# Sample scores of a decoder step: four products with a running sum against one product and one sum along the last axis, and combined output weights made inside the heads' part

## The chip, the cores and the metric

The kernel runs on one core of a Trainium2 chip. The metric is the device time of one execution in microseconds (us). Engines are called as in the profile: PE is the matrix engine, PEld its weight load, DVE the vector engine, ACT the scalar engine, POOL the general one, and SP the engine from whose queue nearly all DMAs are issued. Each engine works through its own list of instructions in order; semaphores hold an instruction back until what it reads is there and what it overwrites has been read.

## The reference

One layer of a hybrid decoder: eight heads of stick-breaking attention and four groups of gated linear attention (GLA) share one input projection and one output projection. There are 1072 tokens: 16 learned meta tokens, a prompt of 1024, and 32 sample tokens (8 sequences of 4). Cut to what the change touches:

```python
def branch_inputs(h, w_in, w_alpha, b_alpha):
    u = h @ w_in
    sq, sk, sv, sg, gq, gk, gv, gg, ga = jnp.split(u, idx, axis=-1)
    ...
    log_f = jax.nn.log_sigmoid((ga @ w_alpha + b_alpha).astype(jnp.float32)) / GLA_TAU

def sb_sample(q, k_new, v_new, k_past, v_past, bias):
    z = jnp.concatenate([sb_logits(q, k_past, bias), sb_logits(q, k_new, bias)], axis=-1)
    ...

def branch_output(o_sb, sg, o_gla, gg, gla_norm_g, w_out):
    ...
    mixed = jnp.concatenate([o_sb * jax.nn.silu(sg), o_gla * jax.nn.silu(gg)], axis=-1)
    return mixed @ w_out
```

`sb_logits(q, k_past, ...)` is the dot product of each sample query (4 tokens in each of 8 sequences and 8 heads, 128 elements) with the 1024 past keys of its sequence. The keys lie in a paged cache: 8 pages of 128 keys for each sequence. So there are 8 heads x 8 sequences x 8 pages = 512 pieces of 128 keys x 128 elements, each met by four queries.

## The kernel before

**Projections.** The fp32 products run as three products of a high and a low part each (L288, L289, L290 in `inproj`). A projection of 128 columns takes eight weight chunks; `weight_chunk` (L176) loads a chunk by a DMA on SP (`wr`, L179), ACT rounds it to the high part (`wh`, L183) and DVE subtracts to get the low part (`wl`, L184), with three buffers each. Each chunk then feeds three column chunks of 384, 384 and 304 tokens with six matmuls each, 18 in all, into three PSUM accumulators (`accp`, three buffers for the whole program, so that a new projection's first matmul waits until ACT or DVE have copied out the old accumulator).

**Order.** The projections are the backbone. After each group of six matmuls `inproj` calls `W.beat()`: the `Weaver` advances every generator that is due, a generator writes a few instructions and yields the number of beats until it is due again. Afterwards a tile scheduler makes each engine's list out of the dependencies, its own modelled times and the priority of each instruction; weight chunks and the evacuation of accumulators are written under `urgent()`. `spread` (and the same lines inside `z_feed`) gives an instruction an ordering dependency, without a semaphore, on the last matmul written (`W.mark`), so that it isn't scheduled much earlier than written.

**Stages**, by the profiled execution: input, norm and transposes until about 75 us; the heads' part until about 790 us (for each of eight heads the projections v, k and q, and the attention over the prompt); `low_rank` (L314), the 16-column projection `ga` that the GLA decays are made of; the gates; the four GLA groups g from about 883 to 1385 us, each with the projections gk, gq, gv_0 and gv_1; more gates; around 1472 to 1720 us the sample tokens' softmax and values with the last gates; and the output projection until the end. Of the GLA part the prediction speaks of: the decay's stage (`al`, `ny`, `e`, L727 to L737), the evacuation of `acc_gk` (L672 to L680) and of `acc_gv` (L684 to L693, into `graw`), the product of `gk` with its decay (L825), and four transposes of it at a time (`tr_k`, L859) which ACT copies to `kd` (L864).

**The two generators of the change** are spawned once head 0 has its projections and run beside everything else:

- `z_feed` (L351) makes the sample scores. For each of the 512 pieces a page `kp` (128 keys x 128 elements) is loaded, up to six ahead into seven buffers, and for each sequence and head the four queries are loaded to all partitions (`qb`, 128 x 4 x 128). Four DVE instructions multiply the page by one query each and sum along the elements at the same time (L386, `accum_out`); the product itself (`jk`) is thrown away. The profile shows each as two rows: the multiplication and a read of the accumulator. A piece every two beats.
- `weight_forms` (L402) makes four of the "combined" weights of the output projection, which multiplies quarters of the matrix in seven products: in 16 tiles `tf` (128 x 4 x 512, one buffer) four DMAs load pieces of the four quarters of `w_out` (L407), four DVE subtractions combine them in place (L411), four DMAs store them to memory (`td`, L414). The yields make 60 beats for each tile, 960 in all. `td` is read again from 1854 us on (L1307).

Of the kernel before, what the change touches and what calls it, by code (L numbers as in the profile page):

```python
# [10 lines left out]
F32 = mybir.dt.float32  # L11
F32R = mybir.dt.float32r
# [4 lines left out]
ALU = mybir.AluOpType  # L17
# [3 lines left out]
P = 128  # L21
# [5 lines left out]
NT = 4  # L27
NSMP = NB * NT
T = META + SEQ + NSMP
# [5 lines left out]
NPG = 8  # L35
# [47 lines left out]
def hybrid_step(ctx: ExitStack, tc: tile.TileContext, x_prompt, x_sample, cache_k, cache_v, state_gla,  # L83
# [23 lines left out]
    W = Weaver()  # L107
# [188 lines left out]
    dk_cm = tc.tile_pool(name="dk", bufs=2, side="right")  # L296
    dk = dk_cm.__enter__()
    wa = []
    ga = dk.tile([96, T], F32R, tag="ga", bufs=1, name="ga")
    walr = dk.tile([96, GH * P], F32, tag="walr", bufs=1, name="walr")  # L300

    def low_rank_weights():
# [11 lines left out]
    def low_rank():  # L314

        acc = [accp.tile([P, 512], F32, tag="acc", name=f"acc_ga_{c}") for c in range(3)]
        for kb in range(0, NK, 4):
            for c, (lo, hi) in enumerate(CHUNKS):
                n = hi - lo
                for k in range(kb, kb + 4):  # L320
                    mm(acc[c][:32, :n], wa[k // 8][:, k % 8, :], hh[k][:, lo:hi], start=(k == 0), stop=False)
                    mm(acc[c][:32, :n], wa[k // 8][:, k % 8, :], hl[k][:, lo:hi], start=False, stop=(k == NK - 1))
                W.beat()
            W.beat()
        for c, (lo, hi) in enumerate(CHUNKS):
            with urgent():
                ps = acc[c][:32, :hi - lo]
                act.copy(ga[0:32, lo:hi], ps)
                act.copy(ga[64:96, lo:hi], ps)
                vec.tensor_tensor(ga[32:64, lo:hi], ps, ga[0:32, lo:hi].bitcast(F32), ALU.subtract)  # L330

    paged = {}

# [11 lines left out]
        done.append(d.ins)  # L345


    heads_ready = []
    z_done = set()

    def z_feed(rate):  # L351

        def pages():
            for h in range(HEADS):
                for b in range(NB):
                    for i in range(NPG):
                        yield h, b, i
        qbs, kps = {}, {}

        def fetch(h, b, i):  # L360
            if i == 0:
                qbs[h, b] = dk.tile([P, NT, P], F32, tag="qb", bufs=2, name=f"qb{b}_{h}")
                nc.sync.dma_start(qbs[h, b][:], qsd[b * NT:(b + 1) * NT, h * P:(h + 1) * P].partition_broadcast(P))
            kps[h, b, i] = dk.tile([P, P], F32, tag="kp", bufs=7, name=f"kp{b}_{h}_{i}")
            page_dma(kps[h, b, i][:], cache_k, b, i, slice(h, h + 1))

        ahead = pages()
        fetched = 0
        zt = None
        for n, (h, b, i) in enumerate(pages()):  # L370
            while h not in heads_ready:
                yield 4
            while fetched < n + 6:
                nx = next(ahead, None)
                if nx is None or nx[0] not in heads_ready:
                    if nx is not None:
                        ahead = itertools.chain([nx], ahead)
                    break
                fetch(*nx)
                fetched += 1  # L380
            if i == 0:
                zt = dk.tile([P, NT, NPG], F32, tag="zt", name=f"zt{b}_{h}")
            kp = kps.pop((h, b, i))
            for t in range(NT):
                jk = dk.tile([P, P], F32, tag="jk", bufs=1, name=f"jk{b}_{h}_{i}_{t}")
                ins = vec.scalar_tensor_tensor(jk[:], kp[:], 1.0, qbs[h, b][:, t, :], ALU.mult, ALU.mult,  # L386
                                         accum_out=zt[:, t, NPG - 1 - i:NPG - i])
                if t == 0 and W.mark is not None:
                    tc.add_manual_dep(ins.ins, W.mark.name, NOSYNC, reason="spread")
            if i == NPG - 1:  # L390
                nc.sync.dma_start(zd[b][:, h * 32:(h + 1) * 32], zt[:].rearrange("p a r -> p (a r)"))
                if h == HEADS - 1:
                    z_done.add(b)
            yield rate(n)

    def spread(ins):

        if W.mark is not None:
            tc.add_manual_dep(ins.ins, W.mark.name, NOSYNC, reason="spread")


    def weight_forms():  # L402
        for k, q in itertools.product(range(8), range(2)):
            t = dk.tile([P, 4, 512], F32, tag="tf", bufs=1, name=f"tf{k}_{q}")
            for i, (r, c) in enumerate(((0, 0), (0, 1), (1, 1), (1, 0))):
                r0, c0 = 1024 * r + k * P, 1024 * c + q * 512
                spread(nc.sync.dma_start(t[:, i, :], w_out[0, r0:r0 + P, c0:c0 + 512]))  # L407
                yield 4
            yield 12
            for i, a, b in ((0, 1, 0), (1, 1, 2), (2, 2, 0), (3, 3, 2)):  # L410
                spread(vec.tensor_tensor(t[:, i, :], t[:, a, :], t[:, b, :], ALU.subtract))  # L411
                yield 4
            for j, i in enumerate((0, 2, 1, 3)):
                spread(nc.sync.dma_start(td[j][:, k, q * 512:(q + 1) * 512], t[:, i, :]))  # L414
                yield 4


    def gate_rest(g, lo, hi, x):
# [226 lines left out]
    with tc.tile_pool(name="gp", bufs=1) as gp, tc.tile_pool(name="gps", bufs=1, space=PSUM) as gps:  # L645
# [73 lines left out]
        def decay(g, cb):  # L719

            gs = slice(g * P, (g + 1) * P)
            raw = walr[:, gs]
            wal = gp.tile([96, P], F32R, tag="wal", name=f"wal{g}")
            act.copy(wal[:], raw)
            vec.tensor_tensor(wal[64:96, :], raw[64:96], wal[64:96, :].bitcast(F32), ALU.subtract)
            for c, (lo, hi) in enumerate(CHUNKS):
                n = hi - lo  # L727
                yield 5
                ps = gps.tile([P, 512], F32, tag="P", bufs=2, name=f"al{g}_{c}")
                mm(ps[:, :n], wal[:], ga[:, lo:hi], start=True, stop=True)  # L730
                ny = stage(f"ny{g}_{c}")[:, :n]
                e = stage(f"e{g}_{c}")[:, :n]
                act.activation(ny, ps[:, :n], AF.Identity, scale=-1.0, bias=nbal[:, g:g + 1])
                vec.tensor_scalar(e, ny, 30.0, None, ALU.min)
                act.activation(e, e, AF.Exp)
                act.activation(e, e, AF.Ln, bias=1.0)
                vec.tensor_tensor(e, ny, e, ALU.max)  # L737
                for i in range(3):
                    a = i * P
                    w = P if 3 * c + i < 8 else 16  # L740
                    k = 3 * c + i
                    out = view(cb, col(k) + (P - 1 if k % 2 else 0), (-1 if k % 2 else 1, w))
                    vec.tensor_tensor_scan(out, ones[:].to_broadcast([P, w]), e[:, a:a + w], 0.0, ALU.mult, ALU.add)
                if hi > REAL:
                    vec.tensor_tensor_scan(cb[:, REAL:T], sm4[:], e[:, REAL - lo:], 0.0, ALU.mult, ALU.add)
                yield 1
# [817 lines left out]
```

## Time and profile before

| | us |
|---|---|
| median of three runs | 2112.36 |
| the three runs | 2115.4, 2111.5, 2112.36 |
| the profiled execution: its own time | 2108.24 |
| its span in the trace | 2106.5 |
| from its first to its last instruction of `weight_forms` (L407 to L414) | 87.4 to 1320.9 |
| mean granted clock of PE in it | 0.995 |

The profile is of one execution, so a sum of its parts is to be set against 2108.24 or 2106.5, not against the median. How busy the engines are in each fortieth of the span (53 us), in tenths, shows where each stage has its limit:

```profile
PE   5999999999999999999999999999999999999998
DVE  6368888889888889899889988877544347453576
ACT  7346555565655547423535335353444326332342
DMA  6234443544444353544353444434776666352485
```

PE is busy in 9 tenths or more of every slice but the first and the last. DVE stands at 8 or 9 tenths while the generators run, and falls to 3 to 7 behind them. A wait is shown as engine, tile, line, "<-" and what ended it, then total us, number and longest us. A row of the timeline is start, duration, engine, line, operation, output<-inputs, shapes, and in brackets the idle time before it and what ended it.

### The profile page before, as it was taken

Reading aid. Unit: us, or ns where it says so; the run is one execution under the profiler, and the core shown is the slowest. Engines: PE = TensorE matmul, PEld = TensorE weight load, DVE = VectorE, ACT = ScalarE, POOL = GpSimd, SP = SyncE. Lnnn points to the kernel's source line nnn. Section 1 sums busy time; section 2 is a strip of 40 time slices with the busy share of each in tenths; the row PEclk is TensorE's granted clock in tenths of the full one; section 3 lists DMA queues with packets and bytes.
Section 4 is the critical chain, followed back from the end, with each engine's and each line's share of the span. In section 5 each row is a group of like instructions: output and inputs, shape, how many; then the busy total and the mean of one; then the engine's idle time right before and its main releaser. Section 6 shows DMA issues by size and latency. Waiting matters only on the chain.

```text
span 2106.5 us, 43298 instructions
## 1 busy us (share of the span) xinstructions
PE 2056.2 (98%) x12546; PEld 1868.4 (89%) x12546; DVE 1569.7 (75%) x6593; ACT 991.8 (47%) x2539; POOL 80.9 (4%) x298
## 2 busy tenths in 40 slices
PE   5999999999999999999999999999999999999998
PEld 4999999999999989999899898998888888777776
DVE  6368888889888889899889988877544347453576
ACT  7346555565655547423535335353444326332342
POOL 0000000100000000020000000000000000000000
PEclk9999999999999999999999999999999999999999
DMA  6234443544444353544353444434776666352485
GB/s 200 72 103 123 132 131 100 144 118 121 139 124 126 108 145 102 156 132 117 110 138 104 123 129 113 107 85 135 244 234 219 224 218 201 127 159 75 130 279 186
DMA packets 378505, 301.96 MB, mean 143 GB/s; under 512 B 50073, under 2 KB 318777, under 8 KB 378265
## 3 DMA queue, kind: packets, MB, share of 16 engines
q1 hardware_dynamic: 376072, 298.91, 48.1%
q8 instruction: 99, 1.62, 0.3%
q14 instruction: 142, 1.16, 0.2%
q10 hardware_dynamic: 2192, 0.27, 0.1%
HBM read 241.75 MB, written 57.31 MB: 142 GB/s over the span
## 4 chain that ended last, share of the span: by engine, by line
PE 84%; DMA 6%; DVE 6%; ACT 2%; issue 1%; SPq 0%; DVEq 0%; POOL 0%; ACTq 0%; POOLq 0%
PE acc_g L288 4%; PE acc_g L290 4%; PE b L1471 4%; PE acc_g L289 4%; PE b L1472 4%; PE b L1473 4%; PE acc_k L288 3%; PE acc_gv L288 3%; PE acc_k L289 3%; PE acc_q L288 3%; PE acc_k L290 3%; PE acc_gv L290 3%; PE acc_gv L289 3%; PE acc_q L289 3%; PE acc_q L290 3%; PE acc_v L288 3%
## 5 line engine op out<-in xcount | busy, mean ns | idle before, releaser
L386 DVE SCALAR_TENSOR_TENSOR jk<-kp,qb 128x128 f32<-128x128 f32 x2048 | 591.6, 289 | 38.9 <-DMA qb<-qsd 1.5
L288 PE MATMUL acc_g<-hT,wh_g 128*128 128x368 f32 (+2 forms) x768 | 251.7, 328 | 0.8 <-ACT gx L442 0.8
L290 PE MATMUL acc_g<-hT,wl_g 128*128 128x368 f32 (+2 forms) x768 | 248.4, 323 | 0.0
L289 PE MATMUL acc_g<-hT,wh_g 128*128 128x368 f32 (+2 forms) x768 | 247.9, 323 | 0.0
L1471 PE MATMUL b<-ring,f 128*128 128x512 f32 x416 | 165.7, 400 | 3.2 <-ACT b L1344 2.0
L386 DVE DVE_READ_ACCUMULATOR jk<-kp,qb 128x1 f32 x2048 | 166.9, 81 | 0.0
L1309 DVE TENSOR_TENSOR ring<-wr,ring 128x512 fp32r<-128x512 f32 x104 | 70.6, 690 | 128.7 <-ACT ring L1308 128.3
L1472 PE MATMUL b<-ring,f 128*128 128x512 f32 x416 | 162.8, 391 | 0.7 <-DVE ring L1309 0.5
L1473 PE MATMUL b<-ring,f 128*128 128x512 f32 x416 | 162.4, 390 | 0.0
L288 PEld LDWEIGHTS acc_g<-hT,wh_g 128*128 128x128 f32 x768 | 145.1, 189 | 12.4 <-issue 10.2
L290 PEld LDWEIGHTS acc_g<-hT,wl_g 128*128 128x128 f32 x768 | 144.9, 189 | 2.0 <-issue 2.0
L289 PEld LDWEIGHTS acc_g<-hT,wh_g 128*128 128x128 f32 x768 | 145.1, 189 | 0.7
L1308 ACT CAST ring<-wr 128x512 fp32r<-128x512 f32 x104 | 64.4, 622 | 159.0 <-DMA wr<-in_w_out_dram 80.6
L288 PE MATMUL acc_gv<-hT,wh_gv 128*128 128x384 f32 (+1 forms) x384 | 129.6, 338 | 0.0
L288 PE MATMUL acc_k<-hT,wh_k 128*128 128x378 f32 (+1 forms) x384 | 127.8, 333 | 0.0
L288 PE MATMUL acc_q<-hT,wh_q 128*128 128x368 f32 (+2 forms) x384 | 125.5, 327 | 0.0
L289 PE MATMUL acc_k<-hT,wh_k 128*128 128x378 f32 (+1 forms) x384 | 125.5, 327 | 0.0
L290 PE MATMUL acc_k<-hT,wl_k 128*128 128x378 f32 (+1 forms) x384 | 125.3, 326 | 0.0
L290 PE MATMUL acc_gv<-hT,wl_gv 128*128 128x384 f32 (+1 forms) x384 | 125.2, 326 | 0.0
L289 PE MATMUL acc_gv<-hT,wh_gv 128*128 128x384 f32 (+1 forms) x384 | 124.6, 325 | 0.0
L289 PE MATMUL acc_q<-hT,wh_q 128*128 128x368 f32 (+2 forms) x384 | 123.8, 322 | 0.0
L290 PE MATMUL acc_q<-hT,wl_q 128*128 128x368 f32 (+2 forms) x384 | 123.6, 322 | 0.0
(441 smaller groups left out, 5398.3 us busy)
## 6 DMA issues: line engine op xcount, KB each, us to landing
kp<-in_cache_k_dram SPq DMA_DIRECT2D x512, 64.0 KB
vr<-in_cache_v_dram SPq DMA_DIRECT2D x64, 512.0 KB
tf<-in_w_out_dram SPq DMA_DIRECT2D x64, 256.0 KB
qb<-qsd SPq DMA_DIRECT2D x64, 256.0 KB
td<-tf SPq DMA_DIRECT2D x64, 256.0 KB
wr_g<-in_w_in_dram SPq DMA_DIRECT2D x128, 128.0 KB
wr<-td SPq DMA_DIRECT2D x64, 256.0 KB
wr<-in_w_out_dram SPq DMA_DIRECT2D x48, 256.0 KB
```

The source lines that it names most:

```text
L288: mm(acc[c][:, :n], wh[:, k2, :], hh[k][:, lo:hi], start=(k == 0), stop=False)
L289: mm(acc[c][:, :n], wh[:, k2, :], hl[k][:, lo:hi], start=False, stop=False)
L290: W.mark = mm(acc[c][:, :n], wl[:, k2, :], hh[k][:, lo:hi], start=False, stop=(k == NK - 1)).ins
L386: ins = vec.scalar_tensor_tensor(jk[:], kp[:], 1.0, qbs[h, b][:, t, :], ALU.mult, ALU.mult, accum_out=zt[:, t, NPG - 1 - i:NPG - i])
L1308: act.copy(wh, r)
L1309: vec.tensor_tensor(wl, r, wh.bitcast(F32), ALU.subtract)
L1471: mm(bk[:], ah, wh, start=first and k == 0, stop=False, skip_group_check=True)
L1472: mm(bk[:], ah, wl, start=False, stop=False, skip_group_check=True)
L1473: mm(bk[:], al, wh, start=False, stop=last and k == 7, skip_group_check=True)
```

## The change

Three things change, with no other line of the kernel.

1. A page's four multiplications with running sum become one DVE multiplication of the page, repeated along a middle axis, with all four queries (`jk` is now 128 x 4 x 128), and one DVE reduction of `jk` along its last axis into the page's column of `zt`. The reads and writes in memory are the same.
2. `weight_forms` yields 2 beats behind each load, subtraction and store instead of 4, and 8 instead of 12 between the loads and the subtractions: 32 beats for each tile, 512 in all. Its loads, subtractions and stores are the same in number and size.
3. `ga` no longer has a buffer of its own: when `weight_forms` has ended, `ga` is allocated in the buffer of `tf`, and `low_rank` runs beats until that has happened before it copies its accumulators out.

```diff
-    ga = dk.tile([96, T], F32R, tag="ga", bufs=1, name="ga")
...
     def low_rank():
...
+        while not ga:
+            W.beat()
+        g = ga[0]
         for c, (lo, hi) in enumerate(CHUNKS):
             with urgent():
                 ps = acc[c][:32, :hi - lo]
-                act.copy(ga[0:32, lo:hi], ps)
-                act.copy(ga[64:96, lo:hi], ps)
-                vec.tensor_tensor(ga[32:64, lo:hi], ps, ga[0:32, lo:hi].bitcast(F32), ALU.subtract)
+                act.copy(g[0:32, lo:hi], ps)
+                act.copy(g[64:96, lo:hi], ps)
+                vec.tensor_tensor(g[32:64, lo:hi], ps, g[0:32, lo:hi].bitcast(F32), ALU.subtract)
...
+    ga = []
...
             kp = kps.pop((h, b, i))
-            for t in range(NT):
-                jk = dk.tile([P, P], F32, tag="jk", bufs=1, name=f"jk{b}_{h}_{i}_{t}")
-                ins = vec.scalar_tensor_tensor(jk[:], kp[:], 1.0, qbs[h, b][:, t, :], ALU.mult, ALU.mult,
-                                         accum_out=zt[:, t, NPG - 1 - i:NPG - i])
-                if t == 0 and W.mark is not None:
-                    tc.add_manual_dep(ins.ins, W.mark.name, NOSYNC, reason="spread")
+            jk = dk.tile([P, NT, P], F32, tag="jk", bufs=1, name=f"jk{b}_{h}_{i}")
+            spread(vec.tensor_tensor(jk[:], kp[:].unsqueeze(1).to_broadcast([P, NT, P]), qbs[h, b][:], ALU.mult))
+            vec.tensor_reduce(zt[:, :, NPG - 1 - i:NPG - i], jk[:], mybir.AxisListType.X, ALU.add)
...
                 spread(nc.sync.dma_start(t[:, i, :], w_out[0, r0:r0 + P, c0:c0 + 512]))
-                yield 4
-            yield 12
+                yield 2
+            yield 8
             for i, a, b in ((0, 1, 0), (1, 1, 2), (2, 2, 0), (3, 3, 2)):
                 spread(vec.tensor_tensor(t[:, i, :], t[:, a, :], t[:, b, :], ALU.subtract))
-                yield 4
+                yield 2
             for j, i in enumerate((0, 2, 1, 3)):
                 spread(nc.sync.dma_start(td[j][:, k, q * 512:(q + 1) * 512], t[:, i, :]))
-                yield 4
+                yield 2
+        ga.append(dk.tile([96, T], F32R, tag="tf", bufs=1, name="ga"))
...
-                mm(ps[:, :n], wal[:], ga[:, lo:hi], start=True, stop=True)
+                mm(ps[:, :n], wal[:], ga[0][:, lo:hi], start=True, stop=True)
```

Because the scheduler's modelled times for the page and for the moved subtractions differ, instructions that the diff doesn't name change places too. PE's list is the same, row for row, through the whole heads' part and again from the later gates on; between them it differs. Behind the first of the changed lines, line numbers are one to three higher than before (L859 becomes L860, L386 becomes L388 for the multiplication and L389 for the reduction). Three places:

**PE where GLA group 0 ends its last projection (gv_1) and the next group's gk begins** (`tr_k` are the transposes of this group's decayed keys, `al` and `o` small products of the decay and of the output; `_0`, `_1`, `_2` behind `acc` are column chunks). Before:

```order
L290 MATMUL acc_gv_1_0_17532<-hT_161,wl_gv_1_7_18008 128x384
L859 MATMUL tr_k_0_18022<-ident,gk_16028 128x128 x4
L288 MATMUL acc_gv_1_1_17533<-hT_160,wh_gv_1_7_18007 128x384
L289 MATMUL acc_gv_1_1_17533<-hT_160,wh_gv_1_7_18007 128x384
L290 MATMUL acc_gv_1_1_17533<-hT_160,wl_gv_1_7_18008 128x384
L288 MATMUL acc_gv_1_1_17533<-hT_161,wh_gv_1_7_18007 128x384
L289 MATMUL acc_gv_1_1_17533<-hT_161,wh_gv_1_7_18007 128x384
L290 MATMUL acc_gv_1_1_17533<-hT_161,wl_gv_1_7_18008 128x384
L859 MATMUL tr_k_4_18059<-ident,gk_16028 128x128 x4
```

With the change:

```order
L290 MATMUL acc_gv_1_2_15950<-hT_161,wl_gv_1_7_16363 128x304
L927 MATMUL o_0_16530<-gv_0_15495,at_15492 128x128
L731 MATMUL al_0_16574<-ga,wal_16474 128x384
L731 MATMUL al_1_16771<-ga,wal_16474 128x384
L860 MATMUL tr_k_0_16377<-ident,gk_14640 128x128 x4
L860 MATMUL tr_k_4_16408<-ident,gk_14640 128x128 x4
L288 MATMUL acc_gk_0_16436<-hT_146,wh_gk_0_16441 128x384
```

The eight transposes stood between the column chunks of gv_1; now they stand behind all of them, directly ahead of the next projection. In the other three groups they have moved behind gv_1 in the same way, with `o` and `al` between the first four and the second four.

**ACT at the same place.** Before:

```order
L183 CAST wh_gk_1_18177<-wr_gk_1_18175 128x256
L689 COPY graw_1_0_18017<-acc_gv_1_0_17532 128x2x128
L693 COPY graw_1_0_18017<-acc_gv_1_0_17532 128x128
L864 COPY kd_18020<-tr_k_0_18022 128x512
L685 COPY graw_1_1_18035<-acc_gv_1_1_17533 128x2x128
L686 COPY graw_1_1_18035<-acc_gv_1_1_17533 128x128
L864 COPY kd_18020<-tr_k_4_18059 128x512
L183 CAST wh_gk_2_18270<-wr_gk_2_18268 128x256
```

With the change:

```order
L825 ACTIVATE ke_16246<-ke_16246 128x1072
L183 CAST wh_gk_2_16602<-wr_gk_2_16600 128x256
L865 COPY kd_16375<-tr_k_0_16377 128x512
L690 COPY graw_1_0_16372<-acc_gv_1_0_15948 128x2x128
L694 COPY graw_1_0_16372<-acc_gv_1_0_15948 128x128
L686 COPY graw_1_1_16389<-acc_gv_1_1_15949 128x2x128
L687 COPY graw_1_1_16389<-acc_gv_1_1_15949 128x128
L692 COPY graw_1_2_16420<-acc_gv_1_2_15950 128x128
```

The copy of the first accumulator (`graw_1_0`), for which the next gk waits, stood ahead of `kd`; now it stands behind the cast of the next chunk's weights and behind `kd`, which needs the transposes.

**ACT between gk and gq of group 0** (`e` is the decay's stage, `X_64` an exponential of 128 x 1024, `wh_gq` the next weights). Before:

```order
L735 ACTIVATE e_2_16426<-e_2_16426 128x304
L736 ACTIVATE e_2_16426<-e_2_16426 128x304
L183 CAST wh_gq_1_16638<-wr_gq_1_16636 128x256
L672 COPY gk_16028<-acc_gk_0_16030 128x256
L673 COPY gk_16028<-acc_gk_0_16030 128x128
L675 COPY gk_16028<-acc_gk_1_16031 128x256
L676 COPY gk_16028<-acc_gk_1_16031 128x128
L782 ACTIVATE X_64_17177<-X_64_17177 128x1024
L678 COPY gk_16028<-acc_gk_2_16032 128x128
L679 COPY gk_16028<-acc_gk_2_16032 128x128
L680 COPY gk_16028<-acc_gk_2_16032 128x48
L183 CAST wh_gq_2_16683<-wr_gq_2_16681 128x256
```

With the change:

```order
L736 ACTIVATE e_2_14989<-e_2_14989 128x304
L737 ACTIVATE e_2_14989<-e_2_14989 128x304
L673 COPY gk_14640<-acc_gk_0_14642 128x256
L674 COPY gk_14640<-acc_gk_0_14642 128x128
L676 COPY gk_14640<-acc_gk_1_14643 128x256
L677 COPY gk_14640<-acc_gk_1_14643 128x128
L183 CAST wh_gq_2_15211<-wr_gq_2_15209 128x256
L679 COPY gk_14640<-acc_gk_2_14644 128x128
L680 COPY gk_14640<-acc_gk_2_14644 128x128
L681 COPY gk_14640<-acc_gk_2_14644 128x48
L183 CAST wh_gq_3_15265<-wr_gq_3_15263 128x256
L783 ACTIVATE X_64_15637<-X_64_15637 128x1024
```

The exponential `X_64` stood ahead of the copies of the third accumulator; it now stands behind them. The stage `e_2` still stands ahead of the copies of the first. One more move, told without rows: on PE the product `Cs` of the sample softmax (L1097) stood in gate projection chunk 6, behind a matmul of its second column chunk; it now stands in chunk 7, in its third column chunk, 24 matmuls further back.

## Prediction

> **What bounds the kernel now.** The page's first row gives the engines' busy time, its chain of waits the work that ended last.
>
> ```profile
> PE 2056.2 (98%) x12546; PEld 1868.4 (89%) x12546; DVE 1569.7 (75%) x6593; ACT 991.8 (47%) x2539; POOL 80.9 (4%) x298
> PE 84%; DMA 6%; DVE 6%; ACT 2%; issue 1%; SPq 0%; DVEq 0%; POOL 0%; ACTq 0%; POOLq 0%
> ```
>
> PE is busy 98% of the span. The change takes work from DVE, at 75%. So DVE's saving counts only where PE waits, and I read the stages next: the table by windows (each row: from, to, length, then busy us and instructions of PE, PEld, DVE, ACT and POOL, then PE's granted clock, DMA share and GB/s).
>
> ```profile
> 180.00:790.00 610.00, 608.71 (x3710) 580.52 (x3709) 533.50 (x2542) 348.56 (x896) 50.53 (x183) 1.00 0.46 126
> 290.00:400.00 110.00, 110.00 (x672) 106.08 (x672) 94.79 (x456) 62.48 (x158) 8.65 (x31) 1.00 0.48 132
> 790.00:1480.00 690.00, 678.79 (x4453) 637.47 (x4452) 607.14 (x3047) 305.18 (x859) 23.00 (x85) 1.00 0.43 121
> ```
>
> In the heads' part (first row) PE stands still 610.00 - 608.71 = 1.3 us, and a stretch of it (second row) shows none at all: there faster DVE work gains nothing. From 790 to 1480 it stands still 11.2 us. The table of PE's waits from 80 to 1500 us names nearly all of that:
>
> ```profile
> PE Cs L1097 <- issue: 2.3, 1, 2.3
> PE acc_gq L288 <- ACT gk L673: 2.2, 1, 2.2
> PE acc_gk L288 <- ACT gx L442: 1.8, 1, 1.8
> PE Us L961 <- DVE km L958: 1.5, 1, 1.5
> PE acc_ga L321 <- DVE q L625: 1.3, 1, 1.3
> PE acc_gq L288 <- ACT gk L680: 1.2, 1, 1.2
> PE tr_v L859 <- DVE pk L851: 0.7, 1, 0.7
> PE z L531 <- DVE lo_s L495: 0.2, 1, 0.2
> ```
>
> These eight are 11.2 us. Nothing else in the kernel's first 1500 us can be won, except what a lower clock adds:
>
> ```profile
> 1480.00:1485.00 5.00, 5.00 (x27) 5.00 (x27) 2.24 (x7) 1.94 (x5) 0.00 (x0) 0.73 0.65 227
> 1485.00:1490.00 5.00, 5.00 (x33) 5.00 (x33) 3.79 (x9) 4.30 (x12) 0.00 (x0) 1.00 0.65 215
> 910.00:915.00 5.00, 3.81 (x18) 3.31 (x18) 5.00 (x20) 3.03 (x7) 0.00 (x0) 0.74 0.33 105
> 883.00:888.00 5.00, 4.63 (x29) 4.63 (x30) 3.53 (x17) 3.51 (x9) 0.00 (x0) 1.00 0.68 174
> ```
>
> Behind the 2.3 us wait for `Cs` the clock is 0.73 for five us: (1 - 0.73) x 5 = 1.4 us. Behind the 2.2 us wait of `acc_gq` it is 0.74 (third row): 1.3 us. Behind the 1.8 of `acc_gk` (fourth row) it stays 1.00.
>
> **The page's work on DVE.** Before, two of the four queries in a row, and a 128x512 product between two other instructions:
>
> ```profile
> 466.44 0.29 DVE L386 SCALAR_TENSOR_TENSOR jk<-kp,qb 128x128 f32<-128x128 f32 x1
> 466.77 0.29 DVE L386 SCALAR_TENSOR_TENSOR jk<-kp,qb 128x128 f32<-128x128 f32 x1
> 1106.84 0.69 DVE L411 TENSOR_TENSOR tf<-tf 128x512 f32<-128x512 f32 x1
> 1107.45 0.28 DVE L386 SCALAR_TENSOR_TENSOR jk<-kp,qb 128x128 f32<-128x128 f32 x1
> L1058 DVE TENSOR_REDUCE zn<-zm 32x32 f32<-32x256 f32 x1 | 0.4, 399 | 0.0
> L1068 DVE TENSOR_REDUCE nmask<-nm 32x4 f32<-32x32 f32 x1 | 0.2, 192 | 0.0
> L1121 DVE TENSOR_TENSOR_SCAN ds<-sm,ds 128x256 f32<-128x256 f32 x1 | 0.7, 692 | 0.0
> ```
>
> A query takes 466.77 - 466.44 = 0.33 us from start to start, a page 4 x 0.33 = 1.33. The product of 128x512 takes 1107.45 - 1106.84 = 0.61. No reduction of 128x512 is in the trace; from the two there are, one element more costs (399 - 192) / (256 - 32) = 0.92 ns, so 512 take 399 + 256 x 0.92 = 636 ns, and 0.56 if its last 0.08 overlap, as the product's do. From above: if it went at the scan's rate, twice 692 ns, 1.38 us. I take 0.60, nearest to the row of the same operation. A page then costs 1.21 instead of 1.33 (1.17 to 1.99): 512 x 0.12 = 61 us less DVE work in all, all of it beside PE. What it costs if that cover goes is a rival below.
>
> The Trainium skill, page "VectorE: DVE Perf Modes", section "Rules for kernel authors", speaks against this: it expects a reduction at the single rate and calls it the slowest DVE operation. By its formula for an fp32 tensor_tensor add of 512, (512 + 151) / 0.96 = 691 ns (an estimate for the reduction; the trace's 690 ns product agrees), the page would be 1.30, and nothing would be won on DVE; the sum below would stay as it is.
>
> **The combined weights, moved.** The same 64 loads, 64 subtractions and 64 stores, earlier:
>
> ```profile
> 180.00:790.00 610.00, 22.02 (x32) 1.00 0.46 126
> 790.00:1480.00 690.00, 19.18 (x28) 1.00 0.43 121
> tf<-in_w_out_dram SPq DMA_DIRECT2D x64, 256.0 KB
> ACT wh_k L183 <- PE acc_k L289: 15.1, 6, 2.6
> ACT wh_v L183 <- DMA kp<-in_cache_k_dram: 3.4, 2, 2.4
> SPq L407 <- DMA td<-tf: 3.5, 3, 2.0
> ```
>
> The first two rows are L411 alone: 28 subtractions come into the heads' part, 28 x 0.61 = 17 us over 610, or 3.1 in 110. That part's pages number (956 products of L386) / 4 = 239, or 43 in 110 us; they give 43 x 0.12 = 5.2 back. DVE there stays at about 93 of 110: cost zero, covered by PE. Seven of 16 tiles' DMAs, 7 x 8 x 256 KB = 14.7 MB, add 24 GB/s to 126; 227 GB/s stand in the row of 1480. The two rows of ACT show that its casts of weights mostly wait for PE and rarely for a DMA, so weights arrive early; zero too. On SP a tile's first load waits for the last tile's stores, with weight loads queued behind it: 2.0 us at most now; two beats come off the gap, and the weights' lead covers it. If it doesn't, that is a rival.
>
> What DVE's tighter schedule could delay on PE in the heads is `lo_s`, the low part that the product `z` reads: 0.2 us of wait now. The last `lo_s` of a head is ready just ahead of PE, and a page on DVE ahead of it would now be one block of 1.21 instead of four that others can go between. I put **+0.8** (eight heads, 0.1 each; 0 to +5, eight times half a page).
>
> **The order behind the heads.** The rows of order shown above move four places on PE's path.
>
> *gk to gq of group 0.*
>
> ```profile
> 906.79 0.46 ACT L735 ACTIVATE e<-e 128x304 f32<-128x304 f32 x1 [5.20 <-issue]
> 908.52 0.45 PE L288 MATMUL acc_gq<-hT,wh_gq 128*128 128x384 f32 x1 [2.16 <-ACT gk L673]
> 911.82 1.06 ACT L782 ACTIVATE X<-X 128x1024 f32<-128x1024 f32 x1 [2.92 <-DVE X L781]
> 913.35 0.41 PE L288 MATMUL acc_gq<-hT,wh_gq 128*128 128x304 f32 x1 [1.19 <-ACT gk L680]
> ```
>
> The 1.19 stands because ACT waits 2.92 for the input of `X_64` with the third accumulator's copies behind it. Now they are ahead: -1.2. The 2.16 stands because `e_2`, ahead of the first copies, waits for DVE; that order is kept, so it stays in the likeliest case or shrinks: -0.6 (0 to -2.2), and the clock's 1.3 with it in half of the cases: -0.6. Together **-2.4** (0 to -4.7).
>
> *Cs.* The wait of 2.3 ends with DVE's chain of the sample softmax. PE now reaches it 24 matmuls later, 24 x 0.17 = 4.1 us (a 384-column matmul follows the next in 0.17); DVE's chain also holds another two weight subtractions. Half of 2.3 + 1.4 and a little more: **-2.2** (0 to -3.7).
>
> *gx to gk, 1.8.* ACT's copies change places; one of three accumulators is free earlier, another perhaps later: **-0.5** (-1.8 to +1).
>
> *gv_1 to the next projection, four times.* New waits come here.
>
> ```profile
> 1119.91 1.27 DVE L825 TENSOR_TENSOR gk<-gk,ke 128x1072 f32<-128x1072 f32 x1
> 1121.24 0.66 PE L859 MATMUL tr_k<-ident,gk 128*128 128x128 f32 x4
> 1121.93 0.59 ACT L864 COPY kd<-tr_k 128x512 f32<-128x512 f32 x1 [0.16 <-PE tr_k L859]
> 1121.23 0.37 ACT L689 COPY graw<-acc_gv 128x256 f32<-128x256 f32 x1 [0.73 <-PE acc_gv L290]
> 1121.50 0.27 ACT L693 COPY graw<-acc_gv 128x128 f32<-128x128 f32 x1
> 1122.78 0.60 PE L859 MATMUL tr_k<-ident,gk 128*128 128x128 f32 x4
> ```
>
> Before, ACT empties the first accumulator (1121.23) as soon as its column chunk ends, before the second transposes (1122.78). Now that copy is queued behind `kd`, and `kd` behind transposes that PE does last. From the start of the transposes: 0.69 to the start of `kd` (1121.93 - 1121.24), 0.59 for it, 0.54 for the two copies: 1.8 us until gk may begin. PE has the transposes themselves and in group 0 the small products in that time, about 1.3: 0.5 idle. Behind it `tr_v` waits some 0.2, and the transposes wait for `gk`'s product (L825) where that is late by a page on DVE, 0.3: 1.0 for a group, 4.0 for four, less the 0.7 of `tr_v` that goes: **+3.3** (+0.5 to +14).
>
> **The sum.** 2108.2 + 0.8 - 2.4 - 2.2 - 0.5 + 3.3 = 2107.2 by the profiled execution. That lies 4.1 us below the median of the runs (2112.4), so the median I forecast is 2107.2 + 4.1 = 2111.3, say **2111.0**: within 0.2% (4.2 us, about what a measurement of this kernel tells from no change).
>
> **Rivals.** *A: the waits go and none come.* For it: the four waits that the order touches (2.3, 2.2, 1.8, 1.2) are 7.5 us, with their clock 10.2. Against: the order at gv_1. If three quarters go and the turn costs 1: 2112.4 - 7.7 + 1 = 2105.7.
>
> *B: the turn of gv_1 costs clock, and the kernel is slower.* Decides from an idle time of about 2 us: the row of 908.52 has a gap of 2.16 with a clock of 0.74 behind it, the gap of 1.8 none. If the product L825 comes a whole page and two weight subtractions later (1.2 + 0.8), a turn idles 0.5 + 0.2 + 2.0 = 2.7 and loses 1.3 of clock: 4 x 4.0 = 16, in place of the +3.3: 2111.3 - 3.3 + 16 = 2124. For it: DVE's new order ahead of L825. Against: DVE's page is shorter.
>
> The Trainium skill, "TensorE: Matmul & The Clock Gate", section "Why this matters for your kernels", asks for no idle gap above about 3 us. By that rule B's turns would lose no clock, 4 x 2.7 = 11 and 2119; the trace, with gaps of 2.16 and 2.34 already followed by 0.74 and 0.73, differs, and decides.
>
> *C: the reduction is slow.* DVE's headroom in 110 us is 110 - 94.8 = 15.2, less 3.1 for the moved subtractions. Over 43 pages that is 0.28 each: from a page of 1.61, a reduction of 1.0, DVE bounds the heads. At the upper end, 1.99, it is (1.99 - 1.61) x 239 = 91 us: 2200. For it: the scan's 692 ns for 256. Against: the slope of the reductions.
>
> *D: the combined weights aren't hidden.* With a tile's loads two beats nearer to the last stores, SP waits longer with weight loads behind: if each of the 16 tiles delays PE by 0.6: +10, 2121. For it: the row of L407. Against: ACT's casts wait for PE.
>
> **How the numbers follow.** The forecast 0.40, A 0.34, B 0.14, C 0.04, D 0.08. So faster by over 0.2% 0.34, within 0.2% 0.40, slower 0.14 + 0.04 + 0.08 = 0.26. The range: below, A with all of 10.2 and nothing new: 2112.4 - 10.2 = 2102, and one more for the other waits, 2101; above, into B and D, 2121. The forecast's own is 2107 to 2115.
>
> **What would show it.** The reduction's row: 0.6 to 0.7 us and PE without idle time from 180 to 790 (else C). No L411 behind `acc_ga`. The waits `gk L681` and `Cs` gone from the table, waits of gk's first matmul for `graw` in its place, about 0.5 each; if those are above 2 and the windows behind show a clock near 0.74, B. More than 5 us at SP's L407, with ACT's casts waiting for DMAs, is D. A stage other than these with over 3 us of change makes the account wrong, whatever the total.

## The result and the profile after

| | median us | against the kernel before, 95% interval |
|---|---|---|
| before (6 runs beside the change) | 2111.93 | |
| changed (6 runs) | 2124.37 | 1.0052 [1.0040, 1.0064] |

The change makes the kernel slower by 0.5%, about 12 us, outside the predicted range (2101 to 2121) and on the side that the forecast gave 0.26. The runs of the changed kernel spread more (2120.4 to 2128.3) than those of before (2110.3 to 2115.4). Its profiled execution took 2128.32, 3.9 above its median; the profiled execution of before lay 4.1 below the median quoted then. So the two spans, 2126.6 and 2106.5, differ by 20, and what both runs and traces bear out is 12 to 16. In the table of the experiments one of the four executions of qb_three, which took 6525.6, is left out.

The page of the changed kernel, busy time of the engines:

```profile
PE 2064.9 (97%) x12546; PEld 1869.1 (88%) x12546; DVE 1663.5 (78%) x3521; ACT 989.2 (47%) x2539; POOL 104.6 (5%) x298
```

DVE's sum rose from 1569.7 to 1663.5, by 94, although work was to be taken from it. Nearly all of it is the sample pages: their rows (L386) covered 608.0 us before, and those of L388 and L389 cover 351.6 + 348.7 = 700.3. What that does to the prediction is told below; the next view is by stages. In the chain that ended last DVE has 9% instead of 6%, DMA 8% instead of 6%.

The table by windows of the changed kernel (columns as in the prediction):

```profile
180.00:790.00 610.00, 600.13 (x3613) 570.48 (x3612) 568.63 (x1098) 345.14 (x880) 65.81 (x178) 1.00 0.51 143
600.00:605.00 5.00, 4.89 (x22) 4.68 (x23) 3.92 (x9) 1.61 (x7) 0.00 (x0) 0.66 0.38 101
790.00:1480.00 690.00, 680.92 (x4461) 634.13 (x4460) 647.28 (x1478) 299.94 (x861) 25.19 (x75) 1.00 0.38 98
```

PE now stands still 9.9 us in the heads' part, where it stood still 1.3; from 790 to 1480 us it stands still 9.1 us instead of 11.2. So the loss is in the stage that was forecast to change by 0.8 us. The first row of `acc_ga`, the projection behind the last head, shows how large it is: first and last start stand behind the durations. Before:

```profile
L321 PE MATMUL acc_ga<-hT,wa x48: 297/334/363, 775.3 to 793.4; 128*32 128x384 f32 x32, 128*32 128x304 f32 x16
```

Changed:

```profile
L320 PE MATMUL acc_ga<-hT,wa x48: 297/333/363, 791.1 to 809.2; 128*32 128x384 f32 x32, 128*32 128x304 f32 x16
```

It begins 15.8 us later. Of that 8.6 is the idle time above, 0.8 more idle time from 80 to 180 us, and 1.7 a lower clock behind one stop (below). The other 4.7 were not taken apart; some of it lies in rows around a stop that count as busy: from 283.5 to 300.2 us PE falls back by 3.0 us against before, with 2.1 of it idle. The output projection's first product (`b`) begins at 1774.6 instead of 1758.9, 15.7 later: between the two places nothing is lost or won. (The last 4 us of this one execution come in the output projection's last 100 us, whose instructions are unchanged.) PE's waits from 75 to 1520 us in the changed kernel:

```profile
PE acc_v L288 <- DVE q L626: 4.0, 2, 2.1
PE z L532 <- DVE lo_s L496: 3.5, 7, 0.7
PE tk_k L462 <- ACT X L528: 2.3, 2, 1.2
PE os L955 <- DMA Sb<-in_state_gla_dram: 2.1, 2, 1.9
PE acc_gq L288 <- ACT gk L674: 1.7, 1, 1.7
PE Cs L1098 <- issue: 1.2, 1, 1.2
PE tr_k L860 <- ACT kd L865: 1.1, 2, 0.7
```

The first three lie in the heads' part. The first and the third are new; the second was 0.2 us before. Each is followed back in turn.

**acc_v, twice about 2 us.** A new head's first projection waits for the copy of `q`'s accumulators, DVE's and ACT's. ACT and DVE around the first of the two, at 219 us:

```profile
215.44 0.51 ACT L488 CAST V<-vr 127x384 fp32r<-127x384 f32 x1 [4.08 <-DMA vr<-out_dram]
218.14 0.47 ACT L625 ACTIVATE q<-acc_q 128x368 fp32r<-128x368 f32 x1
```

```profile
215.99 0.56 DVE L489 TENSOR_TENSOR V<-vr,V 127x384 fp32r<-127x384 f32 x1 [2.84 <-ACT V L488]
218.74 0.53 DVE L626 SCALAR_TENSOR_TENSOR q<-acc_q,q 128x368 fp32r<-128x368 f32 x1
```

ACT stands 4.08 us for `vr`, the head's value rows, which `load_v` reads back from memory; DVE stands 2.84 behind ACT; `q` is copied behind both. SP's queue of before and of the changed kernel at this head:

```profile
197.06 0.44 SPq L482 DMA_DIRECT2D vr<-out_dram  x1
...
199.92 0.41 SPq L484 DMA_DIRECT2D vr<-out_dram  x1
```

```profile
209.84 1.44 SPq L407 DMA_DIRECT2D tf<-in_w_out_dram  x1
212.81 0.38 SPq L483 DMA_DIRECT2D vr<-out_dram  x1
...
217.00 0.37 SPq L483 DMA_DIRECT2D vr<-out_dram  x1
```

Before, all of `vr` was issued by 200 us, 12 us ahead of ACT's use. Now it is behind the loads of a `tf` tile, first issued at 212.8 and last after 217. Behind the second such stop, at 600 us, PE's clock is 0.66 for five us (second row of the windows): another 1.7 us.

**tk_k, twice, 1.2 us and small waits behind.** SP and ACT at 284 to 291 us:

```profile
283.23 0.43 SPq L366 DMA_DIRECT2D qb<-qsd  x1
283.88 0.33 SPq L550 DMA_DIRECT2D od<-ost  x1
```

```profile
289.86 0.39 ACT L536 ACTIVATE Y<-z,bias 127x150 f32<-127x150 f32 x1 [2.70 <-DMA od<-ost]
291.08 0.28 ACT L528 ACTIVATE X<-z 1x150 f32<-1x150 f32 x1
```

`ost`, a head's output, and `Y` use the same three buffers (tag `X`), so this `Y` waits until the store of `ost` has landed, 6.0 us after its issue. Ahead of the store SP had just issued `qb`. Before, the store was issued at 279.85, `qb` only behind it, and `Y` at 283.17 waited for nothing.

**z for lo_s, seven times up to 0.7 us.** DVE in the changed kernel and before, at the same place of the program:

```profile
392.65 0.45 DVE L496 TENSOR_TENSOR lo_a<-Y,hi_a 127x276 fp32r<-127x276 f32 x1
393.02 0.68 DVE L389 TENSOR_REDUCE zt<-jk 128x4 f32<-128x512 f32 x1
393.62 0.57 DVE L496 TENSOR_TENSOR lo_s<-X,hi_s 127x402 fp32r<-127x402 f32 x1
```

```profile
384.80 0.45 DVE L495 TENSOR_TENSOR lo_a<-Y,hi_a 127x276 fp32r<-127x276 f32 x1
385.24 0.58 DVE L495 TENSOR_TENSOR lo_s<-X,hi_s 127x402 fp32r<-127x402 f32 x1
```

A reduction now stands between the two, and PE's wait there, 0.68 us, is the length of the reduction.

### The profile page after: what moved, and what is told of

It is laid out like the page before. It is cut to its first block, busy times and chain, and to the rows that moved or that the text cites. A ratio compares the mean times of both kernels' runs of the same rounds, so it can differ in the third digit from the quotient of the medians.

```text
span 2126.6 us, 40254 instructions
## 1 busy us (share of the span) xinstructions
PE 2064.9 (97%) x12546; PEld 1869.1 (88%) x12546; DVE 1663.5 (78%) x3521; ACT 989.2 (47%) x2539; POOL 104.6 (5%) x298
## 4 chain that ended last, share of the span: by engine, by line
PE 78%; DVE 9%; DMA 8%; ACT 2%; issue 2%; SPq 1%; POOL 0%; DVEq 0%; ACTq 0%; POOLq 0%
PE acc_g L288 5%; PE acc_g L289 4%; PE acc_g L290 4%; PE b L1472 4%; PE b L1473 3%; PE b L1474 3%; PE acc_k L288 3%; PE acc_k L289 3%; PE acc_k L290 3%; PE acc_v L288 3%; PE acc_gv L288 2%; PE acc_gv L289 2%; PE acc_gv L290 2%; PE acc_v L289 2%; PE acc_v L290 2%; PE acc_q L288 2%
## 5 line engine op out<-in xcount | busy, mean ns | idle before, releaser
L388 DVE TENSOR_TENSOR jk<-kp,qb 128x512 f32<-128x512 f32 x512 | 351.6, 687 | 5.6 <-DMA qb<-qsd 2.0
L389 DVE TENSOR_REDUCE zt<-jk 128x4 f32<-128x512 f32 x512 | 348.7, 681 | 4.9
L288 PE MATMUL acc_g<-hT,wh_g 128*128 128x304 f32 (+2 forms) x768 | 252.0, 328 | 1.4 <-ACT gx L443 1.4
L289 PE MATMUL acc_g<-hT,wh_g 128*128 128x304 f32 (+2 forms) x768 | 247.9, 323 | 0.0
```

Source lines behind the costliest of these rows:

```text
L288: mm(acc[c][:, :n], wh[:, k2, :], hh[k][:, lo:hi], start=(k == 0), stop=False)
L289: mm(acc[c][:, :n], wh[:, k2, :], hl[k][:, lo:hi], start=False, stop=False)
L388: spread(vec.tensor_tensor(jk[:], kp[:].unsqueeze(1).to_broadcast([P, NT, P]), qbs[h, b][:], ALU.mult))
L389: vec.tensor_reduce(zt[:, :, NPG - 1 - i:NPG - i], jk[:], mybir.AxisListType.X, ALU.add)
```

## The experiments

Each ratio is against the kernel before on the same chip. The runs come from several chips, where the median of the kernel before lay between 2111.9 and 2114.7, so kernels are compared by their ratios; 0.1% is 2.1 us. "acc_ga" and "b" are the first starts of these two tiles in the profiled execution, with the difference to before (775.3 and 1758.9): what the heads' part lost, and what was lost by the start of the output projection.

| kernel | median us | ratio, 95% interval | acc_ga | b |
|---|---|---|---|---|
| changed | 2124.37 | 1.0052 [1.0040, 1.0064] | 791.1, +15.8 | 1774.6, +15.7 |
| move_only | 2114.73 | 1.0014 [1.0003, 1.0026] | 781.1, +5.8 | 1764.6, +5.7 |
| page_only | 2131.33 | 1.0086 [1.0069, 1.0102] | 784.8, +9.5 | 1780.9, +22.0 |
| before_four_pages | 2117.62 | 1.0022 [1.0012, 1.0032] | 776.4, +1.1 | 1764.9, +6.0 |
| values_first | 2114.54 | 1.0007 [0.9998, 1.0017] | 776.6, +1.3 | 1762.5, +3.6 |
| vr_urgent | 2119.41 | 1.0023 [1.0011, 1.0035] | 785.0, +9.7 | 1766.7, +7.8 |
| ost_own | 2121.58 | 1.0042 [1.0027, 1.0056] | 782.1, +6.8 | 1770.9, +12.0 |
| no_sum | 2113.82 | 0.9994 [0.9982, 1.0006] | 785.1, +9.8 | 1763.2, +4.3 |
| qb_three | 2124.55 | 1.0060 [1.0039, 1.0081] | 788.3, +13.0 | 1774.3, +15.4 |
| no_subtract | 2124.05 | 1.0044 [1.0027, 1.0061] | 790.7, +15.4 | 1774.9, +16.0 |
| move_vr_urgent | 2110.97 | 0.9978 [0.9966, 0.9990] | 776.7, +1.4 | 1762.3, +3.4 |

### One half of the change alone

move_only, the changed kernel with the old page:

```diff
-            jk = dk.tile([P, NT, P], F32, tag="jk", bufs=1, name=f"jk{b}_{h}_{i}")
-            spread(vec.tensor_tensor(jk[:], kp[:].unsqueeze(1).to_broadcast([P, NT, P]), qbs[h, b][:], ALU.mult))
-            vec.tensor_reduce(zt[:, :, NPG - 1 - i:NPG - i], jk[:], mybir.AxisListType.X, ALU.add)
+            for t in range(NT):
+                jk = dk.tile([P, P], F32, tag="jk", bufs=1, name=f"jk{b}_{h}_{i}_{t}")
+                ins = vec.scalar_tensor_tensor(jk[:], kp[:], 1.0, qbs[h, b][:, t, :], ALU.mult, ALU.mult,
+                                         accum_out=zt[:, t, NPG - 1 - i:NPG - i])
...
```

Expected: 

> The changed kernel with the page's four DVE multiplications with running sum put back; the combined weights stay inside the heads' part. Theory Q (queue: the moved loads and stores of the combined weights make SP issue the value rows vr late and the output store od land late, and ACT, then DVE and PE stand behind them): about 2120 to 2125, the stops of 1.1 to 2.1 us at the heads' turns are still there, PE idle 6 us or more from 180 to 790. Rival P (page: blocks of 0.7 us and a multiplication and reduction that wait for each other fill DVE and delay it): within 3 us of the kernel before, 2109 to 2115, PE idle under 3 us in that stretch. Rival S (the moved subtractions fill DVE): as Q in time, but with the stops ended by DVE's busy time, not by ACT's wait for a DMA.

Measured: by the ratio 3 us slower than before, not 8 to 12; the time lies in rival P's range. The longest of PE's waits from 180 to 790 us in this kernel:

```profile
PE acc_v L288 <- DVE q L629: 3.6, 2, 2.0
```

The two stops of `acc_v` are there at full size; those of `tk_k` are not in its list. PE stands still 4.1 us in this window, less than Q said and more than P. Theory Q was right about `vr` and the moved weights, and wrong that they make the whole loss.

page_only puts the old beats and `ga`'s own buffer back instead; before_four_pages is its measure:

```diff
-            kps[h, b, i] = dk.tile([P, P], F32, tag="kp", bufs=7, name=f"kp{b}_{h}_{i}")
+            kps[h, b, i] = dk.tile([P, P], F32, tag="kp", bufs=4, name=f"kp{b}_{h}_{i}")
...
-            while fetched < n + 6:
+            while fetched < n + 3:
```

Expected of page_only: 

> The kernel before with the page as one multiplication and one reduction; the combined weights at their old beats, and ga in its own buffer. To make room, four page buffers instead of seven and three pages ahead instead of six. Theory Q: the turns of the heads show no stop above 0.7 us, so within 4 us of the kernel with four page buffers alone. Rival P: 8 us or more slower than that kernel, with the waits of lo_s and of the turns as in the changed kernel.

Expected of before_four_pages: 

> The kernel before with four page buffers instead of seven and three pages ahead instead of six: the measure for page_only. All theories: 2110 to 2120, since DVE takes 1.33 us for a page and a page comes every 2.6 us.

Measured: page_only 13.7 us above before_four_pages by the medians (both from one chip), as rival P had it, so that Q fell as it stood: the new page alone costs. In the heads it is 9.5 - 1.1 = 8.4 us; with the move's 5.8 that makes 14.2 of the changed kernel's 15.8, so the two halves nearly add. PE's waits in page_only from 180 to 790 us, and the longest from 790 to 1500:

```profile
PE z L532 <- DVE lo_s L496: 2.4, 4, 0.8
PE tk_k L462 <- ACT X L528: 0.9, 1, 0.9
```

```profile
PE tr_k L860 <- DVE gk L826: 5.9, 2, 4.6
```

`tk_k` and `lo_s` come with the page, `acc_v` with the move. The GLA part adds 22.0 - 9.5 = 12.5 us here, 5.9 of it in two waits for the product of `gk` on DVE: the mechanism of the prediction's rival B, in this order of the lists. The changed kernel's own order has no wait above 0.7 us there.

### The two late DMAs taken away

vr_urgent puts `vr`'s loads ahead in SP's list; ost_own gives `ost` a buffer, so that no `Y` waits for its store; values_first has both.

```diff
-                nc.sync.dma_start(sv[1:KT + 1, :nt], src[c * 378:c * 378 + nt * KT].rearrange("(a p) d -> p a d", p=KT))
+                with urgent():
+                    nc.sync.dma_start(sv[1:KT + 1, :nt], src[c * 378:c * 378 + nt * KT].rearrange("(a p) d -> p a d", p=KT))
...
-                st = sp.tile([P, 512], F32, tag="X", bufs=3, name=f"ost{h}_{qi}")
+                st = sp.tile([P, 512], F32, tag="ost", bufs=1, name=f"ost{h}_{qi}")
```

Expected of values_first: 

> The changed kernel with the loads of the value rows vr written as urgent, so that SP's list holds them ahead of the moved loads of the combined weights, and with a buffer of its own for the head's output ost, so that no Y waits for its store. Theory Q: the stops before acc_v and tk_k (about 2 us each, four of them, with the clock behind one) go: 2110 to 2117, what is left being the waits of lo_s. Rivals P and S: no gain beyond 2 us, 2122 to 2126, since DVE is as full as before.

Expected of vr_urgent: 

> The changed kernel with only the loads of the value rows vr written as urgent; ost stays in the buffers of Y. Theory Q, now in two halves: the late vr is the price of the moved weights (move_only has these two stops too), the late store od, which stands right behind the load qb in SP's list, is the price of the page's new order (page_only has that one). Then here the two stops before acc_v go and the two before tk_k stay: 2117 to 2121. Rival (one cause for both, DVE's fullness): either all four stay or all four go.

Expected of ost_own: 

> The changed kernel with only the head's output ost in a buffer of its own; vr stays where it was. Theory Q in two halves: the two stops before tk_k and the waits of z behind them go, the two before acc_v stay: 2118 to 2122. Together with vr_urgent the gains add up to that of values_first, 10 us.

From PE's waits from 180 to 790 us in vr_urgent and in ost_own (values_first has 0.4 us for `lo_s` and no other):

```profile
PE tk_k L462 <- ACT X L529: 2.1, 2, 1.2
```

```profile
PE acc_v L288 <- DVE q L626: 3.1, 2, 1.6
PE z L532 <- DVE lo_s L496: 1.1, 4, 0.5
```

Each edit takes away the stop it was aimed at and leaves the other; with both, the heads' part loses 1.3 us instead of 15.8, and the kernel is level with before to within 0.2%. So without the two late DMAs the change costs next to nothing, with the same page and the same moved subtractions on DVE: DVE's work alone is not the price. The waits for `lo_s` went with them, from 2.7 us to 0.4 between 180 and 790, so what those cost by themselves is not shown. The gains by the ratios, 0.29% for vr_urgent and 0.10% for ost_own, make 0.39 of the 0.45% of values_first. ost_own won 9.0 us in the heads, more than its two stops, because the waits for `lo_s` shrank as well; it gave 5.2 back in the GLA part, so its median gained little.

### How full DVE is

no_sum replaces the reduction by a copy of one element for each query, so the sample scores are not computed; no_subtract leaves out L411, so the output projection gets other weights.

```diff
-            vec.tensor_reduce(zt[:, :, NPG - 1 - i:NPG - i], jk[:], mybir.AxisListType.X, ALU.add)
+            vec.tensor_copy(zt[:, :, NPG - 1 - i:NPG - i], jk[:, :, 0:1])
```

```diff
-            for i, a, b in ((0, 1, 0), (1, 1, 2), (2, 2, 0), (3, 3, 2)):
-                spread(vec.tensor_tensor(t[:, i, :], t[:, a, :], t[:, b, :], ALU.subtract))
-                yield 2
+            yield 8
```

Expected of no_sum: 

> The changed kernel without the sum: the reduction of 128x512 is replaced by a copy of one element for each query, so the sample scores are not computed, and a page takes DVE about 0.7 us instead of 1.3. vr still stands behind the loads of tf and od behind qb in SP's list. Theory Q: the four stops at the heads' turns stay, above 1 us each before acc_v; only the waits of z for lo_s go: 2116 to 2122. Rival P or S (DVE's fullness makes the stops): with 140 us less work on DVE in the heads all of them go: below 2114.

Expected of no_subtract: 

> The changed kernel without the 64 subtractions (L411): the weights are loaded and stored as they are, so the output projection gets other weights; all loads and stores keep their beats. DVE has 34 us less work in the heads' part. Theory Q: vr still stands behind the loads of tf, od behind qb: the four stops stay, 2118 to 2124; rival S (the moved subtractions fill DVE and make the stops): below 2114.

no_subtract came out in time as theory Q had it: no gain beyond the intervals, so the moved subtractions themselves cost nothing that can be measured. Its stops did not all stay, though: `acc_v` has three (3.8 us), but of those of `tk_k` one of 0.3 is left, although ACT still waits 6.0 us for `od` (7.4 in the changed kernel); and PE stands still 8.6 us from 180 to 790, where the changed kernel has 9.9: other waits took their place. no_sum split the theories. The longest of PE's waits from 180 to 790 us in it, and the window of the heads:

```profile
PE acc_v L288 <- DVE q L626: 4.9, 2, 3.1
```

```profile
180.00:790.00 610.00, 602.68 (x3650) 575.24 (x3649) 471.68 (x1115) 348.66 (x886) 58.42 (x179) 1.00 0.52 143
```

DVE is busy 97 us less, and the stops of `acc_v` are as long as ever: not a matter of DVE's fullness, but of the queue. The stops of `tk_k` are gone from the list, against what was expected, although ACT still waits 5.5 us for `od`. As in no_subtract, a late `od` no longer stops PE where DVE has less to do. And its time, 2113.8, is below the 2116 that Q gave and in the range of P and S: with an emptier DVE the heads' part lost 6.0 us less than in the changed kernel, and from `acc_ga` to `b` it won another 5.5 (from +9.8 to +4.3). So the kernel becomes level in two ways, with both DMAs in time (values_first) or with 97 us less work on DVE in the heads (no_sum): the loss comes of late DMAs and a full DVE together. Only the stops of `acc_v` stay as long with the emptier DVE.

### What makes the store late

qb_three gives `qb` a third buffer, so that its load no longer stands directly ahead of those two stores:

```diff
-                qbs[h, b] = dk.tile([P, NT, P], F32, tag="qb", bufs=2, name=f"qb{b}_{h}")
+                qbs[h, b] = dk.tile([P, NT, P], F32, tag="qb", bufs=3, name=f"qb{b}_{h}")
```

Expected: 

> The changed kernel with three buffers for the queries qb instead of two, so that in SP's list qb no longer stands directly ahead of the two stores od behind which PE stopped (the store td four places ahead stays). vr stays late. Theory: od is late because qb's load is ahead of it. Then the two stops before tk_k go or fall under 0.5 us, as with ost_own, and the two before acc_v stay: 2117 to 2122. Rival (the store td ahead of od, so the moved weights, is enough): the stops before tk_k stay at 1 us and more, 2122 to 2126.

From PE's waits from 180 to 790 us, and POOL's row at 295 us:

```profile
PE z L531 <- ACT hi_s L495: 2.8, 2, 1.4
```

```profile
295.17 0.76 POOL L482 MEMSET vr<- 1x384 f32 x2 [4.50 <-DMA out_dram<-st_k]
```

The stops of `tk_k` went, as expected if `qb` delayed the store. The store of `td` still stands 2.2 us ahead of `od` at both places, as in the changed kernel, so `td` by itself does not make `od` late. But the time did not fall: some us later stops of 1.4 us stand before `z`, and ahead of the first of them POOL's memset waits 4.5 us for another store. Removing one late DMA only showed the next. Whether `qb` would delay `od` without `td` beside it stays open, and which DMA POOL's memset truly waited for was not tried.

### A version that beats both

move_vr_urgent is move_only with the urgent loads of `vr`: the old page, and the combined weights in the heads' part.

Expected: 

> The kernel move_only (the old page, the combined weights in the heads' part) with vr urgent. Theory Q: the two stops of 1.6 and 2.0 us and the clock behind the second go, 5 us: 2108 to 2112, level with or a little faster than the kernel before. Rival: no gain, 2113 to 2116, if vr was only the last of several late inputs there.

It is 0.22% faster than before (interval 0.10% to 0.34%). Its heads' part loses 1.4 us by `acc_ga`. The profiled execution took 2114.9, the slowest of its eight and 3.9 above their median, so where the gain lies is not shown. The kernel before with only `vr` urgent was not run, so how much of the gain is due to the moved weights stays open.

## Why the prediction was wrong

**The step that failed** is "The combined weights, moved", where it says "weights arrive early; zero too" and that the gap on SP is covered by "the weights' lead". It looked at one kind of DMA behind the moved ones, the weight chunks, and these were indeed not late (ACT's casts of weights wait for a DMA 2.2 us at the longest, 2.4 before). It did not look at the others in the same queue: `vr`, whose place in SP's list fell behind a `tf` tile's loads. Price: 5.8 us in the heads (move_only), and 0.29% or about 6 us of the whole (vr_urgent against the changed kernel).

**The second failed step** is the page: "61 us less DVE work in all, all of it beside PE". The reduction was taken at 0.60 us and the page at 1.21. Rows of the changed kernel, first a multiplication with another instruction behind it, then one with its own reduction behind it:

```profile
469.92 0.69 DVE L388 TENSOR_TENSOR jk<-kp,qb 128x512 f32<-128x512 f32 x1
470.55 0.42 DVE L184 TENSOR_TENSOR wl_q<-wr_q,wh_q 128x256 fp32r<-128x256 f32 x1
```

```profile
496.68 0.69 DVE L388 TENSOR_TENSOR jk<-kp,qb 128x512 f32<-128x512 f32 x1
497.40 0.69 DVE L389 TENSOR_REDUCE zt<-jk 128x4 f32<-128x512 f32 x1
498.12 0.69 DVE L388 TENSOR_TENSOR jk<-kp,qb 128x512 f32<-128x512 f32 x1
```

Apart, the multiplication takes 0.63 from start to start; directly followed by its reduction each of the two takes 0.72, so a page back to back is 1.44. The page of before was taken at 4 x 0.33 = 1.33, from two queries in a row. But a query gives way sooner when another instruction stands behind it, here after 0.21 us:

```profile
1107.45 0.28 DVE L386 SCALAR_TENSOR_TENSOR jk<-kp,qb 128x128 f32<-128x128 f32 x1
1107.66 0.74 DVE L783 TENSOR_TENSOR X<-X,gq 128x560 f32<-128x560 f32 x1
```

Only 1053 of the 2048 queries have another query directly behind them. So what the page's rows cover, over its pages, comes out the other way: in the window of the heads L386 before, then L388 and L389 with the change:

```profile
180.00:790.00 610.00, 283.99 (x1912) 1.00 0.46 126
180.00:790.00 610.00, 158.05 (x230) 1.00 0.51 143
180.00:790.00 610.00, 156.12 (x230) 1.00 0.51 143
```

That is 283.99 / 239 = 1.19 us for a page before and (158.05 + 156.12) / 230 = 1.37 with the change. From start to start it is 1.18 and 1.30 over the whole trace, about 60 us more where 61 less were forecast.

DVE became fuller: 568.6 of 610 us in the heads instead of 533.5, and 103 of the 110 us from 290 to 400 where the prediction put about 93. What failed with it is "covered by PE": a new order of DVE's and SP's lists came with the page, and it put a reduction ahead of `lo_s` and `qb` ahead of `od`. The term for `lo_s` was +0.8 (0 to +5); the wait measured 3.5. The late `od` was in no term; that it stops PE only beside a full DVE is what no_sum and no_subtract show. Price of the page in the heads: 8.4 us (page_only less before_four_pages).

**What was right.** Most terms behind the heads held in direction, but not their sum: forecast -2.4 - 2.2 - 0.5 + 3.3 = -1.8, and from the first start of `acc_ga` to that of `b` it is 983.6 us before and 983.5 with the change, -0.1. (The window from 790 to 1480 shows 2.1 us less idle time, but it holds other instructions than before: the 1.2 us for `Cs` now lie at 1499.) By its terms: the wait for `gk` before gq fell from 2.2 + 1.2 to 1.7, without a lower clock behind it; `Cs` fell from 2.3 to 1.2; the 1.8 of gx went whole, better than -0.5. The turn of gv_1 cost 1.1 (`tr_k`) and not 4.0: the direction held, the size was over three times too large. Not foreseen was the wait for `Sb`, 2.1 instead of 0.6, with a lower clock behind it. The eight waits that the prediction adds up to 11.2 are not those of its window: the 1.3 of `acc_ga` and the 0.2 of `lo_s` lie ahead of 790, and 1.3 of other waits (`otr`, `Sb`) are left out.

**The rivals.** A happened by half: of its four waits, 7.5 us, 2.9 are left (1.7 and 1.2), but others came. C did not happen: the reduction takes 0.68, and the threshold was 1.0. B's stop did not happen in the changed kernel, and did in page_only. D, given 0.08, is the nearest: it named the moved DMAs on SP and 2121, but it priced delayed weights, 0.6 for each tile, and not the four stops at the heads' turns.

## What to carry to other kernels

When a step with DMAs is moved, list everything that stands behind it in the issuing queue and ask of each when it is needed; the weights had slack, the value rows had none. A buffer shared between a tile that is stored and one that computes can put a store's landing time on the critical path. The cost of a small instruction depends on what stands behind it: take it from the trace as a mean over its real neighbours, not from two of its kind in a row. A change of an instruction's size changes every list that the scheduler writes: a stage with PE at 100% has no room for a better order, but much for a worse one.

## What the runs showed of the hardware

**The clock.** Behind the stop of 1.87 us at 219 the clock stayed 1.00, behind the one of 2.13 us at 600 it was 0.66 for five us. The Trainium skill ("TensorE: Matmul & The Clock Gate", section "Why this matters for your kernels") sets the gap to avoid at about 3 us; here, as in the trace of before, just over 2 us was enough. Near 2 us the length alone does not decide: in the changed kernel the stop of 1.94 for `Sb` at 1457 us was followed by 0.66 for five us, and in vr_urgent one of 2.12 at 917 us by 1.00.

**POOL beside DVE.** In the changed kernel a mask on `Y` (127x102, 0.27 us at 346.6) took 1.60 us; POOL's row and DVE's rows at the same time:

```profile
441.38 1.60 POOL L538 TENSOR_SCALAR_AFFINE_SELECT Y<-Y 127x102 f32<-127x102 f32 x1 [5.06 <-ACT Y L536]
```

```profile
441.57 0.68 DVE L388 TENSOR_TENSOR jk<-kp,qb 128x512 f32<-128x512 f32 x1
442.17 0.68 DVE L411 TENSOR_TENSOR tf<-tf 128x512 f32<-128x512 f32 x1
442.78 0.67 DVE L389 TENSOR_REDUCE zt<-jk 128x4 f32<-128x512 f32 x1
```

It ends at 442.98, 0.20 us after the reduction begins. POOL's busy time in the heads is 65.8 us against 50.5 before. The Trainium skill ("SBUF — State Buffer", section "Who interferes with whom") says that a DVE instruction with two inputs in SBUF holds off a GpSimd instruction that reads SBUF, and that a reduction does not: these rows agree. What it costs this kernel was not tried by itself.
